# Where the background modulation products of layer 1 are placed: in mLSTM's heads, in the output gate and ahead of the output projection

## The chip, the cores and the metric

The kernel runs on one core of a Trainium2 chip. The metric is the device time of one execution in microseconds (us); a lower time is better. A profiled execution leaves a trace: for each engine (TensorE as PE, its weight loads as PEld, VectorE as DVE, ScalarE as ACT, GpSimd as POOL, SyncE's DMA queue as SP) every instruction with its start, its length and what released it. "L153" is line 153 of the kernel.

## What is computed

The reference is a two-layer trunk over 256 latent and 256 context tokens of width 1024. Only what matters here:

```python
sh1, sc1, g1, sh2, sc2, g2 = adaln(c, ada_w[i], ada_b[i])            # silu(c) @ ada_w[i] + ada_b[i], for each layer i
csh1, csc1, cg1, csh2, csc2, cg2 = adaln(c_ctx, ada_w[i], ada_b[i])  # the same for the context's condition
h = rms_norm(x, norm_mix[i]) * (1.0 + sc1) + sh1                     # hc likewise
# layer 0
mq, mk, mv, mo, mg, aq, ak, av = split(h @ ev_w_in)                  # one input projection
ml = mlstm_bidir(...)                                                # 4 heads of width 128, both directions
y = concat([mlstm_output(ml, mo, ml_norm), gqa(...)]) @ ev_w_out     # output gate, then the output projection
x = x + g1 * y
x = x + g2 * hier_moe(rms_norm(x, norm_ffn[i]) * (1.0 + sc2) + sh2)  # 16 experts, 2 for each token
# layer 1: S5 and SSD heads instead of mLSTM and attention, then the same kind of MoE
```

The modulation products `silu(c) @ ada_w` need nothing of the tokens. `ada_w` is 1024 x 6144 for each layer, 25 MB in float32, and takes part in one product with two rows.

## The kernel before

All 512 tokens lie in four tiles of 128 (`NT` = 4). Layer 0 (`layer0`, `even`) runs in stages: input projections of attention and gates, attention, the mLSTM gates, the queries and keys (four blocks), the values (two blocks of 256 columns, "the value stage"), mLSTM, the output gate (two blocks of 256 columns), `fin` (norm and transposes of mLSTM's output), and the output projection (`out_proj0`). Weights of the input projections are loaded in halves of 512 KB into tiles of the tag `w` (L379, five slots), copied on ScalarE to a high part `wh` (L381) and subtracted on VectorE to a low part `wl` (L383), both with two slots; each product is then three matmuls (L87 to L89).

In mLSTM each of the four heads first builds, for both directions, a table of weights from the gates (L533 on PE, L541 and L544 on DVE, the exponential L549 on ACT). It lies in slots of the tag `x` for even heads and in slots of `wh` for odd heads (L534). Then come the score products (L554), their multiplication into the table (L559), the sums over the values (L567) and the normalisation (L569 to L576).

The modulation products are a background generator, `bgw`: layer 0's second and third part (`ada_b(0)`), layer 1's first part (`ada_a(1)`), layer 1's second and third part (`ada_b(1)`). Each part has 16 steps: a step issues one load of `ada_w` of 512 KB into a slot of `w` (L144), and every second step also issues the products of the last two loads (L153), which go into one PSUM tile. Behind the 16 steps of a part of `ada_b` one more step finishes the part: bias on VectorE (L201), four transposes (L208), copies (L212), and a store to DRAM by POOL (L214). There are 84 steps in all. `bg(n)` takes the next n steps, at a raised priority. The tuple `EVEN_BG` says how many at each place, in order: after each of three blocks of the attention and gate projection, after each of four blocks of queries and keys, after each of the two blocks of values, after each of the two blocks of the output gate. `bg()` without a number, between `fin` and the output projection, takes all that is left.

What sets the order: the DMA queue of SP is issued exactly as the program is written (`manual_schedule`), and a load waits in it until its slot is free; the loads behind it wait with it. The instructions of the other engines are ordered by the planner of the tile framework when the kernel is built: by priority, at the time at which it reckons their inputs to be there. On the chip each engine then runs in that fixed order. The tags `hT` (four slots: the modulated input, read by every projection, later mLSTM's transposed output and a block of `w_out`) and `m8` (four slots: queries, keys, values, mLSTM's output; later a block of `w_out`) also take part in the output projection: `out_proj0` loads the first and second block of `w_out` through `w` into `wh` and `wl`, the third into `hT`, the fourth into `m8`.

With the tuple of before, the steps fall so: 1 to 38 in the blocks up to queries and keys, 39 to 50 in the value stage (the end of `ada_a(1)`), 51 to 62 in the output gate, 63 to 84 ahead of the output projection.

Of the kernel before, what the change touches and what calls it, by code (L numbers as in the profile page):

```python
# [325 lines left out]
def e_pieces(d, sb):  # L326

    if d == 0:
        return [(0, sb, 4)]
    return [[(1, 0, 1), (None, 2, 4)], [(0, 0, 4)], [(1, 2, 3)], [(0, 2, 4)]][sb]  # L330


def pairs(d, tb):

    if d == 0:
        return list(range(tb + 1))
    return [[0, 1], [1], [0, 1, 2, 3], [0, 1, 3]][tb]


class Even(Net):  # L340
# [179 lines left out]
            nc.scalar.activation(cols[:, 1, :, d, :], pv[:, 1, :, d, 0:4], AF.Exp)  # L520
        return cols, nM

    def mlstm(self, cols, nM, qT, kT, v1, hh):
        nc = self.nc
        ss = self.sm.tile([128, NT, ML_H], F32, name="mss", bufs=1)
        scr = self.t("scr", [128, 128])
        for h in range(ML_H):
            W = []
            for d in range(2):
                pm = self.ps(tag="a")  # L530
                r = 32 * d + h
                for z in range(2):
                    nc.tensor.matmul(pm, self.identr[:, r:r + 1].to_broadcast([36, 128]), nM[z], start=(z == 0), stop=(z == 1))  # L533
                w = self.const.tile([128, 1280], F32, name=self.nm("mW"), tag="x", bufs=2) if h % 2 == 0 else self.t("wh", [128, 1280])  # L534
                off, where, offs = 0, {}, {}
                for sb in range(4):
                    for m, a, b in e_pieces(d, sb):
                        n = (b - a) * 128
                        o, i0 = w[:, off:off + n], pm[:, a * 128:b * 128]
                        if m is None:  # L540
                            nc.vector.tensor_scalar(o, i0, cols[:, 0, sb, d, h:h + 1], 0.0, op0=ALU.add, op1=ALU.min)  # L541
                        else:
                            mk = (self.m0, self.m1)[d][:, m * 128:m * 128 + n]
                            nc.vector.scalar_tensor_tensor(o, i0, cols[:, 0, sb, d, h:h + 1], mk, op0=ALU.add, op1=ALU.min)  # L544
                        offs[sb, a] = off
                        for tb in range(a, b):
                            where[sb, tb] = off + (tb - a) * 128
                        off += n
                self.lastW = nc.scalar.activation(w[:, :off], w[:, :off], AF.Exp)  # L549
                W.append((w, offs, where))  # L550
            for sb in range(4):
                t0 = 0 if sb < 2 else 256
                s = self.ps([128, T - t0], "a")
                nc.tensor.matmul(s, kT[:, h, sb * 128:(sb + 1) * 128], qT[:, h, t0:T], start=True, stop=True)  # L554
                for d in range(2):
                    w, offs, _ = W[d]
                    for _, a, b in e_pieces(d, sb):
                        n, off = (b - a) * 128, offs[sb, a]
                        nc.vector.tensor_mul(w[:, off:off + n], w[:, off:off + n], s[:, a * 128 - t0:b * 128 - t0])  # L559
            for tb in range(4):  # L560
                pn = self.ps([128, 2, 129], "b")
                for d in range(2):
                    w, _, where = W[d]
                    ks = pairs(d, tb)
                    for j, sb in enumerate(ks):
                        o = where[sb, tb]
                        self.lastP = nc.tensor.matmul(pn[:, d, :], w[:, o:o + 128], v1[:, sb, h, 0:129], start=(j == 0), stop=(j == len(ks) - 1))  # L567
                den = self.sm.tile([128, 3, 2], F32, name=self.nm("den"), tag="den", bufs=4)
                nc.vector.tensor_scalar(den[:, 0, :], pn[:, :, 128], -1.0, None, op0=ALU.mult)  # L569
                nc.vector.tensor_tensor(den[:, 1, :], den[:, 0, :], pn[:, :, 128], op=ALU.max)  # L570
                nc.vector.tensor_tensor(den[:, 0, :], den[:, 1, :], cols[:, 1, tb, :, h], op=ALU.max)
                nc.vector.reciprocal(den[:, 2, :], den[:, 0, :])
                t = self.t("s2", [128, 128])
                nc.scalar.activation(t, pn[:, 0, 0:128], AF.Copy, scale=den[:, 2, 0:1])
                nc.vector.scalar_tensor_tensor(hh[:, tb, h, :], pn[:, 1, 0:128], den[:, 2, 1:2], t, op0=ALU.mult, op1=ALU.add)
                nc.scalar.activation(scr, hh[:, tb, h, :], AF.Square, accum_out=ss[:, tb, h:h + 1])  # L576

        def fin(mixM):
            v = self.sm.tile([128, NT, ML_H], F32, name="mv", bufs=1)
            nc.vector.tensor_scalar(v, ss, 1.0 / 128, EPS, op0=ALU.mult, op1=ALU.add)  # L580
            r = self.sm.tile([128, NT, ML_H], F32, name="mr", bufs=1)
            self.rsqrt(r, v)
            for tb in range(4):
                p = self.ps(tag="b")
                for h in range(ML_H):
                    nc.vector.tensor_scalar(hh[:, tb, h, :], hh[:, tb, h, :], r[:, tb, h:h + 1], None, op0=ALU.mult)
                    nc.tensor.transpose(p[:, h * 128:(h + 1) * 128], hh[:, tb, h, :], self.ident)
                self.split(mixM[0][:, :, tb * 128:(tb + 1) * 128], mixM[1][:, :, tb * 128:(tb + 1) * 128],
                           p.rearrange("p (h t) -> p h t", h=4))
        return fin  # L590

    def even(self, hT, bg):

        nc, src = self.nc, self.a["ev_w_in"][0]
        bg = iter(bg)
# [22 lines left out]
        cols, nM = self.ml_gates(gp)  # L618
# [4 lines left out]
        qT = self.t("m8", [128, ML_H, T])  # L623
        kT = self.t("m8", [128, ML_H, T])
# [11 lines left out]
        v1 = self.t("m8", [128, NT, ML_H, 130])  # L636
# [6 lines left out]
                nc.vector.tensor_copy(v1[:, i, 2 * c:2 * c + 2, 0:128], p.rearrange("p (h d) -> p h d", h=2))  # L643
            self.bg(next(bg))
        hh = self.t("m8", [128, NT, ML_H, 128])
        fin = self.mlstm(cols, nM, qT, kT, v1, hh)
        for c in range(2):
            w = self.in_w(src, 1536 + 256 * c, 1792 + 256 * c)
            for i in range(NT):
# [54 lines left out]
    def layer0(self):  # L704
        with self.phase("E", dict(ps=2, a=2, b=2, o=1, d=1), wh=2, wl=2), self.sub("Eh", hT=4), \
# [12 lines left out]
            self.bgw = chain(self.ada_b(0), self.ada_a(1), self.ada_b(1))  # L718
            mix = self.even(self.h1T(self.h1_tiles(), xT, *self.shsc[0]), EVEN_BG)
            self.out_proj0(mix)  # L720


EVEN_BG = (4, 4, 6, 6, 6, 6, 6, 6, 6, 6, 6)


def rope_table():
# [1475 lines left out]
```

## Time and profile before

| | us |
|---|---|
| median of three runs | 1331.38 (1319.96 to 1343.16) |
| the profiled execution | 1328.82 |
| its span, first to last instruction | 1327.2 |
| mean granted TensorE clock | 0.927 |
| PE busy in the span | 1137.6 |
| DVE busy in the span | 605.8 |

A table of stretches gives, for a stretch of the span, the busy time and number of instructions of each engine, the granted TensorE clock as a share of full speed, the mean busy share of the 16 DMA engines and what they moved. A row of a timeline gives start and length in us, engine, line, operation, output and inputs, how many instructions are merged in it, and in brackets the idle time of the engine before it and what ended it. Waits name who waited, for whom, the total, how many times, and the longest.

### The profile page before, as it was taken

The page shows a single profiled execution, that of the slowest core. Times are in us where ns is not written, and L with a number is a line of the kernel's source. Part 1 is how long each engine was busy: PE and PEld are TensorE (multiplying, and loading weights), DVE is VectorE, ACT ScalarE, POOL GpSimd, SP SyncE. Part 2 cuts the span into 40 slices and gives each one's busy share as a digit, 9 for nine tenths or more (in the row PEclk, how much of TensorE's full clock was granted, in tenths as well). Part 3 has the DMA queues.
Part 4 walks back from the last instruction along what each step waited for, and adds up shares of the span by engine and source line. Part 5 has one row for each costly group of instructions (what it writes and reads, how often), then busy time and mean ns, then how long its engine had stood idle before and what let it go on. Part 6 is the DMA issues. An engine that isn't in the chain of part 4 may idle for free. (4 is left out here: it accounts for less than half of the span.)

```text
span 1327.2 us, 23457 instructions
## 1 busy us (share of the span) xinstructions
PE 1137.6 (86%) x9689; PEld 701.2 (53%) x9689; DVE 605.8 (46%) x1647; ACT 304.1 (23%) x590; POOL 130.0 (10%) x185
## 2 busy tenths in 40 slices
PE   3899998977879599999999966967867789999895
PEld 0575564656579345545665525846756643432221
DVE  2657664186247521837013188799631531211112
ACT  2425441034121111111121134346221211110000
POOL 2002020000300251212101100000000000000000
PEclk8999999999989699999999986988767889999998
DMA  7876136703993899999999742342769859999960
GB/s 275 281 269 237 50 129 223 252 2 120 320 289 123 277 309 363 348 388 352 367 337 335 280 160 66 112 112 61 289 88 199 360 203 412 420 420 420 420 256 34
DMA packets 103973, 330.40 MB, mean 249 GB/s; under 512 B 18049, under 2 KB 56089, under 8 KB 78256
## 3 DMA queue, kind: packets, MB, share of 16 engines
q1 hardware_dynamic: 94592, 298.98, 63.2%
q0 software_dynamic: 9264, 29.81, 7.1%
q8 instruction: 80, 1.31, 0.4%
q14 instruction: 37, 0.30, 0.1%
HBM read 312.68 MB, written 18.01 MB: 249 GB/s over the span
## 5 line engine op out<-in xcount | busy, mean ns | idle before, releaser
L981 PE MATMUL ps<-wa,xT 128*32 128x512 f32 x848 | 167.2, 599 | 0.0
L981 PE MATMUL ps<-wb,xT 128*32 128x512 f32 x608 | 139.3, 594 | 0.0
L87 PE MATMUL ps<-wh,hT 128*128 128x256 f32 (+2 forms) x320 | 93.9, 294 | 6.5 <-ACT wh L381 4.7
L89 PE MATMUL ps<-wh,hT 128*128 128x256 f32 (+2 forms) x320 | 93.1, 293 | 4.0 <-DVE hT L315 4.0
L153 PE MATMUL ps<-w,cT 128*32 128x512 f32 x384 | 67.7, 782 | 28.2 <-DMA w<-in_ada_w_dram 24.2
L88 PE MATMUL ps<-wl,hT 128*128 128x256 f32 (+2 forms) x288 | 83.3, 290 | 1.4 <-DVE wl L383 1.4
L984 PE MATMUL ps<-wa,xT 128*32 128x256 f32 x496 | 82.9, 381 | 0.0
L984 PE MATMUL ps<-wb,xT 128*32 128x256 f32 x480 | 82.3, 380 | 0.0
L989 ACT ACTIVATE s<-ps 64x512 f32<-64x512 f32 (+1 forms) x48 | 23.4, 516 | 247.1 <-PE ps L981 246.6
L87 PE MATMUL ps<-hT,wh 128*128 128x512 f32 (+1 forms) x160 | 61.6, 385 | 14.4 <-DVE xs L1722 11.5
L87 PEld LDWEIGHTS ps<-wh,hT 128*128 128x128 f32 x320 | 62.6, 196 | 15.2 <-issue 6.1
L89 PEld LDWEIGHTS ps<-wh,hT 128*128 128x128 f32 x320 | 62.3, 196 | 15.5 <-issue 8.5
L981 PEld LDWEIGHTS ps<-wa,xT 128*32 128x32 f32 x848 | 45.0, 110 | 37.9 <-issue 24.7
L88 PE MATMUL ps<-hT,wh 128*128 128x512 f32 (+1 forms) x160 | 60.6, 379 | 0.0
L89 PE MATMUL ps<-hT,wl 128*128 128x512 f32 (+1 forms) x160 | 60.2, 377 | 0.2 <-DVE wl L1643 0.2
L88 PEld LDWEIGHTS ps<-wl,hT 128*128 128x128 f32 x288 | 55.2, 192 | 7.8 <-issue 5.9
L970 DVE COPY xT<-ps 128x384 f32<-128x384 f32 x16 | 8.9, 556 | 105.9 <-PE ps L984 98.3
L981 PEld LDWEIGHTS ps<-wb,xT 128*32 128x32 f32 x608 | 38.6, 110 | 21.8 <-issue 7.7
L1027 POOL DMA_INDIRECT yd<-y,si x30 | 34.5, 1149 | 155.6 <-ACT y L1018 150.2
L1275 DVE COPY aT<-ps 128x256 f32<-128x256 f32 x16 | 6.8, 424 | 89.3 <-PE ps L1273 89.3
L981 PE MATMUL ps<-wc,xT 128*32 128x512 f32 x288 | 46.5, 595 | 0.0
L87 PEld LDWEIGHTS ps<-hT,wh 128*128 128x128 f32 x160 | 31.8, 199 | 23.5 <-issue 15.7
(659 smaller groups left out, 2387.9 us busy)
## 6 DMA issues: line engine op xcount, KB each, us to landing
w<-in_ada_w_dram SPq DMA_DIRECT2D x96, 512.0 KB
wa<-in_moe_w_down_dram SPq DMA_DIRECT2D x30, 1024.0 KB
wa<-in_moe_w_up_dram SPq DMA_DIRECT2D x28, 1024.0 KB
wa<-in_moe_w_gate_dram SPq DMA_DIRECT2D x25, 1024.0 KB
wb<-in_moe_w_gate_dram SPq DMA_DIRECT2D x21, 1024.0 KB
wb<-in_moe_w_down_dram SPq DMA_DIRECT2D x17, 1024.0 KB
wb<-in_moe_w_up_dram SPq DMA_DIRECT2D x16, 1024.0 KB
w<-in_ev_w_in_dram SPq DMA_DIRECT2D x16, 512.0 KB
```

Of the source, the lines that this page charges most:

```text
L87: mm(p, x[0], y[0], start=first, stop=False)
L88: mm(p, x[0], y[1], start=False, stop=False)
L89: return mm(p, x[1], y[0], start=False, stop=last)
L153: o, i = nc.tensor.matmul(p[32 * q:32 * q + 32, :], self.cT[:, k, :], rhs, start=(k == 0), stop=(k == KD - 1)), o
L970: nc.vector.tensor_copy(xT[:, 0:4, :], p)
L981: self.up = nc.tensor.matmul(P[32 * j:32 * j + 32, :], xT[:, k, 32 * (j % 2):32 * (j % 2) + 32], (wg, wu)[j // 2](k), start=(k == 0), stop ...
L984: nc.tensor.matmul(Q[32 * j:32 * j + 32, :], xT[:, k, 64:96], (wg, wu)[j // 2](k)[:, (j % 2) * 256:(j % 2) * 256 + 256], start=(k == 0), s ...
L989: nc.scalar.activation(s, p[0:64, :], AF.Silu)
L1027: st = self.nc.gpsimd.indirect_dma_start(out=rows, out_offset=bass.IndirectOffsetOnAxis(ap=idx, axis=0), in_=y, in_offset=None, bounds_che ...
L1275: nc.vector.tensor_copy(aT, tr)
```

## The change

The function `mlstm` gets the iterator over `EVEN_BG` and takes background steps in each head, after the tables of both directions and before the score products. The tuple has four more entries: six steps in each of the four heads, then four instead of six after each block of the output gate. The steps up to the value stage are as before (1 to 50); 51 to 74 now fall in mLSTM, 75 to 82 in the output gate, and the last two ahead of the output projection. Steps 67 and 84 are the finishing steps of layer 1's second and third part.

```diff
-    def mlstm(self, cols, nM, qT, kT, v1, hh):
+    def mlstm(self, cols, nM, qT, kT, v1, hh, bg):
...
                 self.lastW = nc.scalar.activation(w[:, :off], w[:, :off], AF.Exp)
                 W.append((w, offs, where))
+            self.bg(next(bg))
             for sb in range(4):
...
-        fin = self.mlstm(cols, nM, qT, kT, v1, hh)
+        fin = self.mlstm(cols, nM, qT, kT, v1, hh, bg)
...
-EVEN_BG = (4, 4, 6, 6, 6, 6, 6, 6, 6, 6, 6)
+EVEN_BG = (4, 4, 6, 6, 6, 6, 6, 6, 6, 6, 6, 6, 6, 4, 4)
```

## Rows read from the trace of the kernel before

**Rows 1.** The page's group of the modulation products: busy, mean ns, idle before, releaser.

```profile
L153 PE MATMUL ps<-w,cT 128*32 128x512 f32 x384 | 67.7, 782 | 28.2 <-DMA w<-in_ada_w_dram 24.2
```

**Rows 2.** Table of stretches: mLSTM, a part of it, the gate, the projection's start.

```profile
core 0: us, PE busy (x) PEld busy (x) DVE busy (x) ACT busy (x) POOL busy (x), PEclk, DMA share, GB/s
266.00:316.10 50.10, 39.34 (x207) 29.57 (x205) 39.86 (x148) 20.55 (x52) 0.00 (x0) 0.93 0.00 1
277.00:288.00 11.00, 10.18 (x50) 7.84 (x49) 8.29 (x32) 4.41 (x11) 0.00 (x0) 0.84 0.00 0
316.10:355.00 38.90, 35.86 (x279) 25.62 (x279) 12.77 (x40) 8.71 (x18) 15.29 (x22) 1.00 0.85 288
363.00:377.00 14.00, 7.78 (x37) 5.91 (x29) 5.28 (x7) 3.14 (x3) 1.17 (x2) 0.51 1.09 312
```

**Rows 3.** Timeline of SP's queue from 220 to 380 us.

```profile
233.22 4.69 SPq L379 DMA_DIRECT2D w<-in_ev_w_in_dram  x2
238.00 18.39 SPq L144 DMA_DIRECT2D w<-in_ada_w_dram  x6
256.49 5.03 SPq L379 DMA_DIRECT2D w<-in_ev_w_in_dram  x2
261.62 97.46 SPq L144 DMA_DIRECT2D w<-in_ada_w_dram  x26
...
360.17 17.26 SPq L379 DMA_DIRECT2D w<-in_ev_w_out_dram  x12
```

**Rows 4.** Waits of SP's queue from 262 to 320 us.

```profile
SPq L144 <- DVE den L572: 55.5, 1, 55.5
```

**Rows 5.** Timeline of PE in the value stage: the modulation products.

```profile
247.43 1.07 PE L153 MATMUL ps<-w,cT 128*32 128x512 f32 x8
...
254.95 1.07 PE L153 MATMUL ps<-w,cT 128*32 128x512 f32 x8 [2.84 <-DMA w<-in_ada_w_dram]
...
260.04 1.06 PE L153 MATMUL ps<-w,cT 128*32 128x512 f32 x8 [0.43 <-DMA w<-in_ada_w_dram]
```

**Rows 6.** Groups by line of PE from 316.5 to 353.6 us.

```profile
L153 PE MATMUL ps<-w,cT 128*32 128x512 f32 x72 | 9.6, 604 | 1.6 <-DMA w<-in_ada_w_dram 1.6
```

**Rows 7.** Timeline of PE from the gate's first product to the projection's first matmul.

```profile
322.94 1.06 PE L153 MATMUL ps<-w,cT 128*32 128x512 f32 x8 [1.39 <-DMA w<-in_ada_w_dram]
...
353.62 0.49 PE L587 MATMUL ps<-ident,m 128*128 128x128 f32 x3
...
362.65 1.53 PE L153 MATMUL ps<-w,cT 128*32 128x512 f32 x8 [2.37 <-DMA w<-in_ada_w_dram]
...
365.71 1.11 PE L208 MATMUL ps<-ident,ab 128*128 128x128 f32 x4 [1.53 <-DVE ab L205]
...
370.83 0.58 PE L87 MATMUL ps<-wh,hT 128*128 128x256 f32 x1 [4.01 <-ACT wh L381]
```

**Rows 8.** Timeline of DVE: the finishing of a part, and the splits after the gate.

```profile
338.30 0.68 DVE L201 TENSOR_TENSOR ab<-ab,ps 128x512 f32<-128x512 f32 x1
...
356.31 1.28 DVE L82 TENSOR_TENSOR hT<-ps,hT 128x512 fp32r<-128x512 f32 x2
...
359.94 0.69 DVE L82 TENSOR_TENSOR hT<-ps,hT 128x512 fp32r<-128x512 f32 x1 [0.89 <-ACT hT L81]
```

**Rows 9.** Waits of PE from 363 to 500 us.

```profile
PE ps L966 <- DMA xg<-h2d,gi: 5.7, 1, 5.7
PE ps L87 <- ACT wh L381: 5.1, 2, 4.0
...
PE ps L88 <- DVE wl L383: 1.6, 2, 0.9
```

**Rows 10.** Timeline of PE in mLSTM's third and fourth head: the sums.

```profile
300.49 5.03 PE L567 MATMUL ps<-m,mW 128*128 128x129 f32 x28 [1.29 <-DVE m L575]
...
307.95 0.94 PE L567 MATMUL ps<-m,wh 128*128 128x129 f32 x6 [0.71 <-DVE m L575]
...
312.66 3.39 PE L567 MATMUL ps<-m,wh 128*128 128x129 f32 x28 [1.77 <-DVE m L575]
```

## The prediction

> **What bounds the kernel now.** I first read the page: the modulation products (L153) are a small part of TensorE's work, but of its costly groups the one whose idle time is put down to a weight load [rows 1]. Then the table of stretches: in mLSTM (266 to 316.1 us) the DMA engines move nothing and PE is idle for 10.8 of 50.1 us; in the output gate (316.1 to 355) DMA is at 0.85 and PE all but full; in 363 to 377 DMA is saturated and PE half idle at a granted clock of 0.51 [rows 2]. The order of SP's queue says why. The output gate's weights are issued at 233.22 and 256.49, then one load of `ada_w` at 261.62, and the other 25 of that batch only after a stall [rows 3]. The stall is one wait of 55.5 us for a slot of `w` [rows 4]: four of its five slots hold output-gate weights, whose split copies need `wh`, which the odd heads of mLSTM occupy to the end. The fifth slot holds half a pair.
>
> A pair, below, is two loads of 512 KB and their eight matmul records (two for each matmul of the source), 1.07 us of PE. Before mLSTM three pairs of layer 1's second modulation part run [rows 5], though their products are written behind mLSTM: the planner already carries a product as far forward as its loads allow, so the place in SP's queue decides. The other 13 pairs run afterwards: nine (72 records) between 316.5 and 353.6 [rows 6], four up to 364, the last of them at 362.65 [rows 7]. Only then have `w_out`'s loads been issued, at 360.17 [rows 3], and the output projection starts at 370.83, after a wait of 4.01 us for the copy that such a load feeds [rows 7].
>
> **The change, step by step.** It changes no work, only the place of loads and pairs: 24 background steps (23 loads) go into mLSTM, 8 instead of 12 into the output gate, 2 (one load) instead of 22 ahead of the projection. In SP's queue the gate's loads now stand behind 23 more loads of `ada_w`, and `w_out`'s behind one.
>
> (a) *From the end of the gate's matmuls to the projection.* Today 353.62 to 370.83 = 17.2 us [rows 7]. It holds four pairs, a wait of 2.37 for a load, 1.53 and 1.11 for the transposes of the finished part, and the 4.01. What must stay is the split of the gated token blocks on VectorE: the first ends at 357.0 (356.31 plus half of 1.28), the last at 360.63 [rows 8], so 3.4 to 7.0 us. One block is enough for the first matmul; I take 3.7: **-13.5** (-13.8 to -10.2).
>
> (b) *Output gate.* Nine pairs, 9.6 us, lie in it [rows 6]. How many remain? After mLSTM's 23 loads SP has: gate weights (2), 4 loads, gate weights (2), 4, then 1. As today, four gate halves and a load that lacks its partner will fill the five slots and SP will stop; so 27 loads go out before the stop and 5 after it, and 3 pairs remain, 3.2 us. The first wait of 1.39 [rows 7] stays, the other 0.2 of 1.6 [rows 6] goes: **-6.6** (-4.5 with two more pairs left, -9.8 with none).
>
> (c) *Early projection.* TensorE waits 5.1 us for two copies, of which 4.01 is in (a), and 1.6 for two subtractions [rows 9], so 2.7 beyond (a). In 363 to 377 it computes 7.78 us at a clock of 0.51 [rows 2], of which 1.2 is the last pair and 1.1 the transposes; the other 5.5 would be 2.8 at 1.00. With `w_out`'s loads out by 330 or so, up to 5.4 us could go, but the second block's copy and subtraction still need slots that the gate reads to its end: **-2.5** (0 to -5.4).
>
> (d) *The value stage, up to 266.* Loads go on from 233.22 without the gate's weights in between, which took SP until 238.00 [rows 3], and with all five slots; so the first pair can come 4.8 us before today's 247.43 [rows 5]. In the gate, nine pairs from 322.94 to 353.6 are one in 3.4 us [rows 6, 7]. From 242.6 to 269 that is 8 pairs instead of 3. PE is saturated there apart from load waits of 2.84 and 0.43 [rows 5], so five pairs cost 5.4 in full; the waits go, since the slots no longer stop the loads: **+2.1** (0 to +5.4).
>
> (e) *mLSTM.* 16 - 8 - 3 = 5 pairs, 5.3 us of PE. Ahead of its runs of L567 a head has waits of 1.29 (1.77 in the last) and 0.71 us [rows 10], in which a pair can hide; elsewhere a pair holds up a chain in which VectorE and TensorE wait for each other, VectorE being busy 39.86 of 50.1 us [rows 2]. I take half, 2.7, plus the 0.68 of L201 [rows 8], a VectorE addition at the end of a part, which now falls there: **+3.4** (-2.6, the pairs hidden and the second rival's gain, to +6.0).
>
> Queues: POOL, which loads a part's bias and stores the part, does nothing in mLSTM [rows 2], and neither does DMA. The diff leaves the order of PE and DVE to the planner. Behind the projection nothing swallows an earlier start: the first expert product waits 5.7 us for the gather of its tokens, not for weights [rows 9].
>
> Sum: -13.5 - 6.6 - 2.5 + 2.1 + 3.4 = -17.1 us. The profiled execution takes 1328.82 us, its span 1327.2 and the rest around it; that gives 1311.7. The median of the runs is 2.6 us higher, which would give 1314; I put the forecast at **1312**.
>
> **The rivals.**
>
> *Little gain.* The pairs cost their full time, and the projection's weights come late: (d) +5.4, (e) +6.0, (a) -10.2, (b) -6.6, (c) 0, together -5.4, **1324**. For it: VectorE's 39.86 of 50.1. Against: the waits of 1.29 and 0.71, and DMA idle for 50 us.
>
> *More gain.* The pairs vanish in mLSTM's waits and PE keeps its clock. Of two runs of 28 records of L567 one took 3.39 us and one 5.03, after a wait of 1.29 [rows 10]; the granted clock is 0.84 on the mean of 277 to 288 [rows 2], where another such run lies, so part of it at 1.2 and not 2.4 GHz. Two runs give back 3.3. Then (e) is 0.7 - 3.3 = -2.6, (d) 0, (c) -5.4: with (a) and (b) -28.1, **1301**. The Trainium skill (TensorE: Matmul & The Clock Gate, Part 1) says that half rate is the resting state and that activity lifts it; by that rule denser work in mLSTM would bring this case. The trace agrees as far as the slow run follows a pause, but the run of 3.39 follows a longer one of 1.77 and is not slow.
>
> *Slower.* PE runs in order: a pair whose load is late stops mLSTM's matmuls behind it, and VectorE with them. At the dearest such wait, 2.84 us [rows 5], for all 10 pairs moved it is 28.4 on top of the forecast, **1340**. It decides from 17.1 / 10 = 1.7 us for a pair. Against: with the loads queued without gaps, the gate's nine pairs waited 1.6 us in all [rows 6]. The same page (Part 3, The mechanism) says that matmuls start and end strictly in program order, which speaks against this change; the waits in front of L153 agree, since nothing overtakes them.
>
> *No effect.* The projection's start is held by something else, such as `w_out`'s last two blocks, which go into slots that the gate reads to its end, or the five slots of `w` move the stall elsewhere: **1329**. For it: the gate's weights still fill four slots until mLSTM ends; against: only five loads of `ada_w` are left then.
>
> That all 12 pairs of the 23 loads run in the value stage is no rival: PE pays 10 x 1.07 = 10.7 there, less 3.3, and (e) is 0, 2 us more than the forecast.
>
> **How the numbers follow.** Forecast 0.52 (its own range 1304 to 1319), little gain 0.20, more gain 0.16, slower 0.06, no effect 0.06. The range 1300 to 1326 holds the forecast, little gain and most of more gain. Two per cent, about what a measurement of this kernel tells from no change, is 26.6 us: faster means below 1304.8, where more gain and a little of the forecast lie, 0.19; slower means above 1358, 0.02; between, 0.79.
>
> **What would show it.** After mLSTM about five loads of `ada_w` instead of 25; about eight pairs before mLSTM, five in it, three after; mLSTM at most 7 us longer than 50; the projection within 4 us of the gate's last matmul, with `w_out` issued before 335. If L554 or L567 stand behind waits for `ada_w`, or mLSTM grows by over 12 us, (e) is wrong; if the projection still waits over 2 us for a copy, (a) is.

## The result, and the profile after

The changed kernel takes 1309.84 us (median of four runs, 1302.33 to 1314.74) against 1330.08 for the kernel before in the same comparison (four runs, 1319.96 to 1343.16). The ratio is 0.9861, with a 95% interval of 0.982 to 0.9903: faster by 1.4%, which the interval tells apart from no change, and less than the 2% that the prediction used as a bound. The profiled execution takes 1311.75 us; the forecast was 1312. The lines of the changed kernel are one higher than before from L550 on (L567 is now L568).

SP's queue shows the change itself. These are its loads from 218 to 354 us in the kernel after:

```profile
218.05 4.73 SPq L379 DMA_DIRECT2D w<-in_ev_w_in_dram  x2
222.88 52.56 SPq L144 DMA_DIRECT2D w<-in_ada_w_dram  x29
278.03 0.93 SPq L379 DMA_DIRECT2D w<-in_ev_w_in_dram  x2
281.64 8.62 SPq L144 DMA_DIRECT2D w<-in_ada_w_dram  x4
294.16 0.93 SPq L379 DMA_DIRECT2D w<-in_ev_w_in_dram  x2
321.21 5.08 SPq L144 DMA_DIRECT2D w<-in_ada_w_dram  x5
...
327.32 26.61 SPq L379 DMA_DIRECT2D w<-in_ev_w_out_dram  x12
```

Where [rows 3] had six loads of `ada_w` between the gate's weights and 26 behind them, 29 now run ahead of them (six for the steps of the value stage, 23 for those of mLSTM), four between, and five are left when the stall ends. `w_out` begins to go out at 327.32 instead of 360.17. The stall of [rows 4] is there still, behind the same instruction, but at under half its length, and it now falls where only five loads stand behind it (waits of SP's queue, 240 to 345 us):

```profile
SPq L144 <- DVE den L573: 26.1, 1, 26.1
```

PE's products of `ada_w` in the value stage, mLSTM and the gate (timeline of PE):

```profile
246.30 1.06 PE L153 MATMUL ps<-w,cT 128*32 128x512 f32 x8
...
257.00 1.07 PE L153 MATMUL ps<-w,cT 128*32 128x512 f32 x8 [0.41 <-DMA w<-in_ada_w_dram]
...
288.34 1.06 PE L153 MATMUL ps<-w,cT 128*32 128x512 f32 x8 [1.10 <-DMA w<-in_ada_w_dram]
...
293.05 1.07 PE L153 MATMUL ps<-w,cT 128*32 128x512 f32 x8
...
332.59 1.06 PE L153 MATMUL ps<-w,cT 128*32 128x512 f32 x8 [0.81 <-DMA w<-in_ada_w_dram]
```

Seven pairs stand in the value stage (246.30 to 267.28), six in mLSTM (270.40 to 293.05), three in the gate, none behind it; the forecast was 8, 5 and 3. The sums of mLSTM that answer to [rows 10]:

```profile
305.39 3.39 PE L568 MATMUL ps<-m,mW 128*128 128x129 f32 x28 [1.29 <-DVE m L576]
...
315.91 3.39 PE L568 MATMUL ps<-m,wh 128*128 128x129 f32 x28 [1.77 <-DVE m L576]
```

Both take 3.39 us here; the first was 5.03 before. Then the end of the gate and the start of the projection, which answer to [rows 7]:

```profile
348.75 1.03 PE L588 MATMUL ps<-ident,m 128*128 128x128 f32 x8
350.86 0.38 PE L87 MATMUL ps<-wh,hT 128*128 128x256 f32 x1 [1.08 <-ACT hT L81]
...
352.71 0.39 PE L88 MATMUL ps<-wl,hT 128*128 128x256 f32 x1 [1.23 <-DVE wl L383]
...
353.72 0.36 PE L89 MATMUL ps<-wh,hT 128*128 128x256 f32 x1
```

The projection starts 2.1 us after the gate's last product instead of 17.2. Two rows of the table of stretches, mLSTM and the gate, stand against [rows 2]; the granted clock is 1.00 in both:

```profile
269.29:319.30 50.01, 42.97 (x261) 28.32 (x260) 40.78 (x151) 20.51 (x52) 5.41 (x9) 1.00 0.52 171
319.30:348.75 29.45, 27.14 (x222) 23.89 (x222) 15.82 (x42) 10.38 (x19) 12.43 (x16) 1.00 0.95 267
```

Routing, the first work of layer 0's MoE that waits for every token, starts 23.3 us earlier (the products L867, then L868, by line; first and last start are the two numbers ahead of the semicolon). First the kernel before:

```profile
L867 PE MATMUL ps<-sel,ones x13: 174/174/175, 446.8 to 1064.9; 128*128 128x16 bf16 x13
```

and after:

```profile
L868 PE MATMUL ps<-sel,ones x13: 173/174/177, 423.5 to 1046.3; 128*128 128x16 bf16 x13
```

But the end comes only 17.1 us earlier (span 1327.2 and 1310.1). Of 23.3 us, 6.9 are given back in the experts of that MoE, where the change moves no work: from the first to the last transposed token block they last 456.1 to 727.0 = 270.9 us before, and 432.8 to 710.6 = 277.8 after. The waits of PE in this stretch say where. Before:

```profile
PE ps L966 <- DVE xT L970: 3.9, 5, 1.2
```

After:

```profile
PE ps L967 <- DVE xT L971: 8.2, 5, 5.3
PE ps L967 <- DMA xg<-h2d,gi: 5.6, 1, 5.6
```

The wait for the gather is that of [rows 9]; the one for the copy of tokens on VectorE has grown, by a single wait of 5.3 us. VectorE's timeline shows what stands ahead of that copy. Before:

```profile
487.11 0.18 DVE L1383 TENSOR_SCALAR ea<-s5ld 128x32 f32<-128x32 f32 x1 [8.99 <-DMA s5ld<-in_s_log_dt_dram]
...
491.90 0.56 DVE L970 COPY xT<-ps 128x384 f32<-128x384 f32 x1 [1.45 <-PE ps L984]
```

After:

```profile
469.01 0.46 DVE L1384 TENSOR_SCALAR ea<-s5ld 128x32 f32<-128x32 f32 x1 [15.00 <-DMA s5ld<-in_s_log_dt_dram]
...
472.40 0.55 DVE L971 COPY xT<-ps 128x384 f32<-128x384 f32 x1
```

L1384 belongs to layer 1: it begins the table of an exponential (`exp_acc`), and its input `s5ld` comes with two small loads that POOL issues at the start of layer 0's MoE (`odd_loads`, L1443). In VectorE's fixed order this table stands ahead of the copy of the fourth expert's tokens. Before, the load lands early enough that the copy still waits 1.45 us for PE; after, it lands later, and PE waits for the copy.
The Trainium skill (TensorE: Matmul & The Clock Gate, Part 1, Architectural detail) says that VectorE takes its work strictly first in, first out. The trace agrees: the copy starts 3.4 us after the table's first instruction, and not during the 15.00 us ahead of it.

### The profile page after: what moved, and what is told of

Its sections match the earlier page's. It is cut to its first block, busy times and chain, and to the rows that moved or that the text cites. A ratio compares the mean times of both kernels' runs of the same rounds, so it can differ in the third digit from the quotient of the medians.

```text
span 1310.1 us, 23459 instructions
## 1 busy us (share of the span) xinstructions
PE 1132.7 (86%) x9689; PEld 694.0 (53%) x9689; DVE 605.2 (46%) x1647; ACT 304.1 (23%) x590; POOL 131.0 (10%) x185
## 5 line engine op out<-in xcount | busy, mean ns | idle before, releaser
L87 PE MATMUL ps<-wh,hT 128*128 128x256 f32 (+2 forms) x320 | 93.7, 294 | 3.6 <-ACT hT L298 1.8
L89 PE MATMUL ps<-wh,hT 128*128 128x256 f32 (+2 forms) x320 | 92.4, 291 | 4.0 <-DVE hT L315 4.0
L153 PE MATMUL ps<-w,cT 128*32 128x512 f32 x384 | 67.2, 777 | 25.2 <-DMA w<-in_ada_w_dram 20.9
L87 PE MATMUL ps<-hT,wh 128*128 128x512 f32 (+1 forms) x160 | 61.5, 384 | 14.2 <-DVE xs L1723 11.6
L89 PEld LDWEIGHTS ps<-wh,hT 128*128 128x128 f32 x320 | 61.8, 194 | 14.5 <-issue 7.7
L87 PEld LDWEIGHTS ps<-wh,hT 128*128 128x128 f32 x320 | 62.4, 195 | 11.3 <-issue 6.1
L89 PE MATMUL ps<-hT,wl 128*128 128x512 f32 (+1 forms) x160 | 60.0, 375 | 0.2 <-DVE wl L1644 0.2
L87 PEld LDWEIGHTS ps<-hT,wh 128*128 128x128 f32 x160 | 31.6, 197 | 23.3 <-issue 15.7
```

The lines of the kernel that those rows point to most:

```text
L87: mm(p, x[0], y[0], start=first, stop=False)
L89: return mm(p, x[1], y[0], start=False, stop=last)
L153: o, i = nc.tensor.matmul(p[32 * q:32 * q + 32, :], self.cT[:, k, :], rhs, start=(k == 0), stop=(k == KD - 1)), o
```

## Experiments

Two theories were to be told apart at first: that the stages gain as forecast and the pairs in mLSTM cost about half their time, or that their cost there is full or none; then, with the traces at hand, what the loss in the experts is. The table has the stages of all traces: the end of the value stage, the lengths of mLSTM and gate, the time from the gate's last product to the projection's first, the length of the experts, the pairs in value stage, mLSTM and behind it, and how many of mLSTM's runs of 28 sums, whole or in part, went at half the clock (5.03 instead of 3.39 us).

| kernel | value end | mLSTM | gate | to projection | experts | pairs | runs at half clock |
|---|---|---|---|---|---|---|---|
| before | 265.35 | 50.70 | 37.57 | 17.21 | 270.9 | 3/0/13 | 2 |
| b2_before | 264.42 | 50.70 | 37.32 | 16.86 | 271.2 | 3/0/13 | 2 |
| b3_before | 267.63 | 52.91 | 38.40 | 17.06 | 271.1 | 3/0/13 | 2 to 3 |
| before_copy_first | 264.70 | 50.02 | 37.28 | 16.80 | 271.2 | 3/0/13 | 1 |
| after | 269.29 | 50.01 | 29.45 | 2.11 | 277.8 | 7/6/3 | 0 |
| a2_after | 268.43 | 50.37 | 29.60 | 2.12 | 277.9 | 7/6/3 | 0 |
| a3_after | 269.09 | 51.55 | 28.98 | 2.12 | 273.8 | 7/6/3 | 1 |
| head0 | 269.89 | 51.84 | 29.25 | 2.12 | 275.3 | 7/6/3 | 1 |
| after_copy_first | 268.13 | 51.52 | 28.63 | 2.12 | 270.8 | 7/6/3 | 1 |
| gate_only | 266.87 | 53.62 | 35.38 | 5.50 | 271.6 | 4/4/8 | 2 |
| all_mlstm | 268.27 | 54.43 | 24.44 | 2.70 | 275.4 | 7/9/0 | 1 |
| all_copy_first | 269.12 | 52.86 | 24.44 | 2.79 | 270.8 | 7/9/0 | 0 |
| twice5 | 267.99 | 58.27 | 30.13 | 2.12 | 271.5 | 7/6/3, five twice | 0 |

**Does the place within mLSTM matter? (head0)** All 24 steps are given in the first head.

```
-EVEN_BG = (4, 4, 6, 6, 6, 6, 6, 6, 6, 6, 6, 6, 6, 4, 4)
+EVEN_BG = (4, 4, 6, 6, 6, 6, 6, 6, 6, 24, 0, 0, 0, 4, 4)
```

> All 24 mLSTM steps taken in the first head (24, 0, 0, 0, 4, 4) instead of six in each. Theory: only the place in SP's queue counts, and that queue is the same; the built program has the same instructions in the same order on every engine as the changed kernel, so it is also its second measurement: 0.986 of before, 1305 to 1315 us, seven pairs in the value stage, six in mLSTM, three behind. Rival (the place in the heads matters): not the same stage lengths. On the loss at the MoE's start, chance: the wait of 5.3 us in front of the second expert is 0 to 3 us here; systematic: 4 to 7 us again.

1310.85 us, ratio 0.9846 (0.9787 to 0.9904). The planner puts the pairs where it reckons their loads to be there, and both tuples give the same instructions in the same order on every engine. So "six in each head" is only a way of writing: what counts is that the loads are issued ahead of the gate's weights. The run serves as a repeat of the changed kernel.

**The gate alone. (gate_only)** No steps in mLSTM, 16 after each block of the gate, two steps (one load) left for the place ahead of the projection, as in the changed kernel.

```
+EVEN_BG = (4, 4, 6, 6, 6, 6, 6, 6, 6, 0, 0, 0, 0, 16, 16)
```

> No step in mLSTM, 16 after each block of the output gate, two ahead of the projection: the loads are only moved from behind the gate to within it. Theory (the order in SP's queue decides): 16 loads go out behind the first block's weights with three slots, so about eight pairs run before mLSTM's end, then four slots are held and SP stops; eight pairs remain for the gate and 15 loads stand ahead of w_out instead of five. mLSTM about 50 us, the gate about 5 us longer than in the changed kernel, the projection's start 4 to 8 us later: 1316 to 1322 us, half of the gain. Rival (what counts is that mLSTM itself takes steps): no gain, 1325 to 1333 us.

1318.19 us, ratio 0.9919 (0.9886 to 0.9953). SP's queue in this kernel:

```profile
240.03 40.81 SPq L144 DMA_DIRECT2D w<-in_ada_w_dram  x16
...
286.17 59.21 SPq L144 DMA_DIRECT2D w<-in_ada_w_dram  x16
...
346.47 21.10 SPq L379 DMA_DIRECT2D w<-in_ev_w_out_dram  x12
```

Even without a step in the heads four pairs run in mLSTM, since the first block's 16 loads go out from 240 us on. But the 16 loads behind the second block's weights are caught in the stall, `w_out` follows at 346.47, eight pairs lie behind mLSTM, and the projection waits 5.5 us. All but emptying the place ahead of the projection, with half of the loads ahead of the second block's weights, brings 11 us in the comparison's medians (1329.25 to 1318.19); the other loads ahead of the gate's weights bring the rest.

**All in mLSTM. (all_mlstm)** 34 steps in the heads, none in the gate.

```
+EVEN_BG = (4, 4, 6, 6, 6, 6, 6, 6, 6, 9, 9, 8, 8, 0, 0)
```

> All 34 remaining steps in mLSTM (9, 9, 8, 8), none in the gate or ahead of the projection. Theory: seven or eight pairs in the value stage, eight or nine in mLSTM, none behind it; four gate halves then hold four slots, and w_out's first half the fifth. The gate loses its three pairs (3.2 us) and its wait of 0.8, w_out's loads are issued some 5 us earlier; mLSTM grows by under 1 us a pair: 3 to 5 us less than the changed kernel, 1304 to 1308. Rival (mLSTM has no more room): its length grows by 3 us or more and the gate's gain is given back: 1309 to 1312.

1307.37 us, ratio 0.9829 (0.9774 to 0.9884). No load of `ada_w` is left behind the gate's weights:

```profile
222.34 68.93 SPq L144 DMA_DIRECT2D w<-in_ada_w_dram  x38
...
312.76 37.87 SPq L379 DMA_DIRECT2D w<-in_ev_w_out_dram  x12
```

The gate is 5 us shorter than after, and mLSTM, with nine pairs, 2.9 (all_copy_first) to 4.4 longer. The difference to the changed kernel is within the intervals.

These runs price a pair in mLSTM. With 1.64 us (5.03 less 3.39) taken off for each run at half clock (b3_before, where part of one more is hit, is left out), mLSTM without pairs takes 47.4 to 48.4 us, with six 49.9 to 50.4, with nine 52.8 to 52.9. Six cost 1.5 to 3.0 and nine 4.4 to 5.5, which is 0.25 to 0.6 us a pair of its 1.07, and of the six's cost 1.1 to 1.6 are waits for loads. The four of gate_only cost 2.0 to 3.0, up to 0.75 a pair, but theirs wait 3.3 us for loads.

**Five pairs more. (twice5)** Of layer 1's third part, the products of pairs 1 to 5 are issued twice (640 of the weight's 1024 rows, those whose number leaves 1 to 5 when divided by 8, then count twice in it), with no load added.

```
+                    for _ in range(2 if l == 1 and v == 2 and 1 <= k <= 5 else 1):
                         o, i = nc.tensor.matmul(p[32 * q:32 * q + 32, :], ...), o
```

> The changed kernel with five pairs of products issued twice (rows 128 to 767 of the third modulation part count twice in the product, which is left so): 5 x 1.07 = 5.4 us more of PE, nearly all of it in mLSTM, with no load more. If a pair hides in mLSTM as the stage lengths say (six pairs made it 50.0 and 51.8 us long against 50.7, with one or two runs of the sums at the full clock instead of the half: some 0.4 us a pair), mLSTM is 51 to 54 us, and the kernel 1 to 3 us slower than the changed one. If a pair costs its full time there, mLSTM is 55 to 57 us and the kernel 5 us slower.

mLSTM takes 58.27 us, 7.9 to 8.4 more than with six single pairs at equal clock. Four of the five doubled pairs stand in mLSTM, at 275.62, 279.00, 288.73 and 294.60; the fifth stands in the gate, at 331.78. A doubled pair lasts 1.95 us instead of 1.07, so the four add 3.5 us of products. The rest is not the products' own: two of the doubled pairs stand in PE's order ahead of their loads (timeline of PE in twice5, where L153 is L154):

```profile
288.73 1.95 PE L154 MATMUL ps<-w,cT 128*32 128x512 f32 x16 [2.73 <-DMA w<-in_ada_w_dram]
...
294.60 1.95 PE L154 MATMUL ps<-w,cT 128*32 128x512 f32 x16 [2.02 <-DMA w<-in_ada_w_dram]
...
331.78 1.95 PE L154 MATMUL ps<-w,cT 128*32 128x512 f32 x16
```

Those waits are 4.75 us, against 1.1 to 1.6 with single pairs. Without the difference, 3.1 to 3.7, the doubled products cost 4.2 to 5.3 us: more than all of their time. So the run does not repeat the price of 0.25 to 0.6 a pair. Either the pauses of mLSTM take in the first products and none of the next, or the planner, which orders PE anew around longer products, put them in worse places; the run doesn't tell which. It does show the mechanism of the rival "slower", a late load in an ordered queue, at 2 to 3 us for a pair. Its whole time can't be told from that of the kernel after (1311.87, ratio 0.986, 0.9819 to 0.9901); its experts, at 271.5 us, give back part of what mLSTM loses, and the next point is about that.

**The loss in the experts: chance or the change?** Nothing is moved there, so further executions of the same kernels were profiled.

> The kernel before once more, for a second trace of it. The changed kernel gained 23.3 us up to the routing of layer 0's MoE, but only 16.4 were left behind its first two experts: there the second expert's matmuls waited 5.3 us for a copy that VectorE did late, behind instructions that waited for small loads. Theory A (chance): how late those loads land varies from execution to execution; then this trace has another wait in front of the second expert than the 0.7 us of the first trace, or the next run of the changed kernel has another than 5.3. Theory B (systematic): the kernel before waits under 1.5 us there every time, and its first expert block takes 17.5 us again from one expert's transposes to the next.

> The changed kernel again, one look. The experts' stretch was 277.8 and 275.3 us in its two traces, 270.8 with the edge of order. If the loss belongs to the change, it is 274 us or more again; if it is chance, 270 to 272 here or 274 and more in a trace of before.

> The changed kernel, a further look with the same question: experts' stretch 274 us or more (belongs to the change) or 270 to 272 (chance); mLSTM 50.0 to 51.8 us, with no run or one of the sums at the half clock.

> The kernel before, a third look. If the loss belongs to the change, its experts' stretch is 270 to 272 us once more, with a wait of 1.2 us for the copy; if it is chance, it is sometimes 274 or more. In mLSTM, two runs of the sums at the half clock again (50.7 us) if that follows from the pauses of PE; one or none if it varies.

The whole times were 1322.52 (b2_before), 1310.35 (a2_after), 1302.55 (a3_after) and 1326.82 (b3_before). Before, the experts take 270.9 to 271.2 us in three executions; after, 277.8, 277.9 and 273.8, and 275.3 in head0. The two groups don't meet, so in these traces the loss goes with the change. The wait behind it varies, and follows one quantity: when POOL issues the second load of `s5ld`, counted from the first transposed tokens.

| kernel | second load of `s5ld` issued after, us | longest of that wait of PE, us | experts, us |
|---|---|---|---|
| before | 25.0 | 0.7 | 270.9 |
| b3_before | 26.1 | 1.2 | 271.1 |
| b2_before | 26.4 | 0.7 | 271.2 |
| gate_only | 26.5 | 1.4 | 271.6 |
| twice5 | 26.8 | 1.6 | 271.5 |
| all_mlstm | 27.8 | 2.8 | 275.4 |
| a3_after | 27.8 | 3.2 | 273.8 |
| head0 | 28.0 | 2.8 | 275.3 |
| after | 30.3 | 5.3 | 277.8 |
| a2_after | 30.8 | 5.5 | 277.9 |

Up to about 26.8 us next to nothing is lost; from there PE waits a us for each us. The stretch doesn't lose just the wait: against the kernel before it is 6.9 us longer for a wait of 5.3 in the kernel after, 4.5 for 2.8 in all_mlstm and 2.9 for 3.2 in a3_after. Behind the wait the granted clock is 0.78 over 20 us in the kernel after, against 1.00 behind the same copy before (table of stretches, before and then after; 0.83 in all_mlstm, 0.91 in a3_after):

```profile
492.50:512.50 20.00, 19.43 (x215) 11.97 (x218) 3.53 (x7) 2.10 (x5) 5.91 (x9) 1.00 1.01 358
```

```profile
472.75:492.75 20.00, 19.75 (x189) 9.13 (x192) 2.21 (x5) 1.06 (x2) 6.93 (x11) 0.78 0.89 305
```

**Take away what makes the copy wait. (before_copy_first, after_copy_first, all_copy_first)** The first instruction of the table is told to come behind the copy of the fourth expert's tokens, in VectorE's order alone; no work changes. In the edit, `hold` is that copy (`xTc`).

```
+                self.xTc = self.ao[-1] if len(self.gat) == 3 else getattr(self, "xTc", None)
...
-        nc.vector.tensor_scalar(t[0], x, -87.0, 87.0, op0=ALU.max, op1=ALU.min)
+        self.after(nc.vector.tensor_scalar(t[0], x, -87.0, 87.0, op0=ALU.max, op1=ALU.min), *hold)
```

> The changed kernel with one edge of order more: VectorE's work on layer 1's tables, which waits for small loads that POOL issues at the MoE's start, is put behind its copy of the fourth expert's tokens instead of ahead of it. Theory: the changed kernel loses up to 7 us there (its stretch from the first to the last token transposes of the experts was 277.8 and 275.3 us in two traces, 271.0 and 271.2 in the kernel before), because VectorE stands in that wait while the copy is ready; then PE's wait for the copy (5.3 and 2.8 us) falls under 1.5, the clock stays at 1.00, and the stretch is 270 to 272 us: 4 to 6 us less than the changed kernel, 1303 to 1308. Rival (the loss is in the weights' loads, which compete with the small ones): another wait takes its place, the stretch stays at 275 to 278, 1308 to 1312.

> The same edge of order in the kernel before. Theory: its two traces show waits of only 1.2 us there, so there is nothing to gain: 0.997 to 1.003 of before, stretch 270 to 272 us. If it gains 4 us or more, the loss belongs to both kernels and varies by chance, and the two traces of before were lucky.

> All 34 steps in mLSTM together with the edge of order. Theory: both gains add: 1300 to 1305, 0.980 of before or less; mLSTM 53 to 55 us, the gate 24 to 25, the stretch of the experts 270 to 272. Rival: the stretch stays at 275, 1304 to 1309.

VectorE in after_copy_first; the copy comes first, and the table's start no longer matters to PE:

```profile
470.42 0.56 DVE L971 COPY xT<-ps 128x384 f32<-128x384 f32 x1 [7.28 <-PE ps L987]
471.95 0.17 DVE L1386 TENSOR_SCALAR ea<-s5ld 128x32 f32<-128x32 f32 x1
```

And PE's waits in its experts:

```profile
PE ps L967 <- DVE xT L971: 3.3, 4, 1.2
```

The second `s5ld` load goes out 29.5 us after the first tokens here, as late as in the changed kernel, and the experts take 270.8 us. The changed kernel with this edit takes 1302.0 us (ratio 0.9823, 0.9758 to 0.9888). That is 7.8 below the changed kernel's median, but the two stem from different comparisons, and by their ratios (0.9823 and 0.9861, whose intervals overlap) it is 5 us. From the last token block to its end the kernel, with nothing moved there, takes anything from 588.7 to 600.4 us in these traces. What shows the effect is the experts' length, 3.0 to 7.1 us shorter than in the traces of the changed kernel, and not the whole time. The kernel before gains nothing from it that can be told (1327.48, ratio 0.9981, 0.9942 to 1.002), as its three traces lose nothing there. But in before_copy_first the second `s5ld` load goes out 27.9 us after the first tokens, 2.9 us later than in the trace of before, and 2.1 of these are there at 472.41, ahead of the first instruction that the edit moves (482.11). By the table above PE would have waited some 3 us for so late a load in the unedited order (an estimate), so the kernel before isn't safe from the loss either. So the loss is VectorE's order together with the late load, and it is mended without touching the change. With all steps in mLSTM as well it takes 1299.94 us (ratio 0.9786, 0.9723 to 0.985), the lowest median of the study.

Why the small loads come later can be followed one step back. POOL issues them in order behind other small loads, some of which wait for expert weights (`wb`) or a gather (`xg`) to land. POOL's timeline before:

```profile
471.15 0.82 POOL L1442 DMA_DIRECT2D LL<-in_s_b_im_dram  x1 [1.67 <-DMA wb<-in_moe_w_down_dram]
472.47 0.81 POOL L1442 DMA_DIRECT2D LL<-in_s_b_im_dram  x1 [0.50 <-DMA xg<-h2d,gi]
```

and after:

```profile
445.62 0.82 POOL L1443 DMA_DIRECT2D LL<-in_s_b_im_dram  x1 [1.04 <-DMA wb<-in_moe_w_down_dram]
449.32 0.82 POOL L1443 DMA_DIRECT2D LL<-in_s_b_im_dram  x1 [2.88 <-DMA wb<-in_moe_w_down_dram]
452.73 0.82 POOL L1443 DMA_DIRECT2D LL<-in_s_b_im_dram  x1 [2.58 <-DMA xg<-h2d,gi]
```

These waits are 2.2 us before and 6.5 after, 4.3 of the 5.3 us by which the second `s5ld` load is later in this pair of traces (30.3 less 25.0). Why the weights and the gather land later in the kernel after, relative to the first tokens, stays open; no run moved them.

## Why the prediction came out, point by point

The steps against the traces; the last column has the means of the four traces of the kernel before (before_copy_first is the same up to the experts) and of five of the kernel after (with head0 and after_copy_first). For the experts the kernels with the VectorE edit are left out.

| step | forecast | the two profiled executions | means |
|---|---|---|---|
| (d) up to the end of the value stage | +2.1 (0 to +5.4) | +3.9 | +3.4 |
| (e) mLSTM | +3.4 (-2.6 to +6.0) | -0.7 | 0.0 |
| (b) gate | -6.6 (-9.8 to -4.5) | -8.1 | -8.5 |
| (a) gate's end to projection | -13.5 (-13.8 to -10.2) | -15.1 | -14.9 |
| (c) projection | -2.5 (-5.4 to 0) | -3.3 | -1.9 |
| sum up to routing | -17.1 | -23.3 | -21.8 |
| the experts | 0 | +6.9 | +5.1 |

**The number was right by two errors that cancel, which is luck.** The sum up to routing was 5 to 6 us too small, most of it in (e), and the sentence "Behind the projection nothing swallows an earlier start" was wrong: the experts swallow 5 to 7. It rested on [rows 9], PE's waits up to 500 us in the kernel before. They show the gather's 5.7 us rightly, but PE's wait for the copy is only 0.7 us long before, and its length doesn't tell that it is on the edge. What would have shown it is VectorE's timeline: an instruction that waits 8.99 us for a small load, five us ahead of a copy that PE needs. What the experts give back, put at nothing, is the term that failed.

**(a)** was mis-sized, 3.7 us where 2.1 was measured. I took half of VectorE's split of the first token block for the condition. The first matmul (L87) needs the high part alone, which ScalarE's L81 gives; only L89 needs the split, and comes at 353.72, 5 us after the gate's end. It lies a little outside its bounds.

**(b)** had the mechanism and the number of pairs right: five loads behind the stall, three pairs. Six pairs fewer are 6.4 us and the waits for loads fall from 1.6 to 0.8. The other 0.9 us comes from the gate's own 192 matmuls. From each start to the next, without waits, they take 25.2 us with nine pairs among them (before), 23.9 with three (after) and 23.0 with none (all_mlstm), and a pair takes 1.00. So in the gate, where PE is all but full, a pair costs some 1.24 us, 0.24 of it in the matmuls beside it.

**(c)** lies within its bounds, but its size is mostly the clock. From its first matmul to routing the projection's stretch takes 75.3 to 76.2 us in the four traces of the kernel before, and after 72.7 (after, a2_after), 74.0 (a3_after) and 75.3 (head0, after_copy_first). In its first 15 us the granted clock is 0.77 to 0.85 before, and after 1.00, 0.89 and 0.77 in that order. The waits for copies and subtractions, of which 2.7 us were to go, are still 1.4 in the kernel after.

**(d)** was counted as 8 pairs against 3 and is 7, the first at 246.30, one in about 3.5 us, as the nine of [rows 6, 7] had been. Of the 3.9 us between the two traces 2.0 were there long before it: a pair of an earlier stage starts at 224.81 instead of 222.76 (1.1 of the 3.4 on the mean). The other 1.9 are the stage's own: four pairs more are 4.3 us, and the waits for their loads fall from 3.3 [rows 5] to 0.4.

**(e)** The half was a fair guess for the pairs: at equal clock the stage grows by 1.5 to 3.0 us with six pairs, where 3.4 was forecast with five. But in the two profiled executions mLSTM got shorter, since the kernel before had two runs of sums at half the clock and the one after none: 3.3 us, as the rival "more gain" had it. The size of that varies from execution to execution: head0, a3_after and after_copy_first, which run the same order up to there, each have one such run. But it isn't chance alone: the four traces of the kernel before have seven or eight of them, the five of the kernel after three, and the first run of 28 in mLSTM, slow in three of the four, is at the full clock in all of the five. On the mean that is about 2 us, as much as the pairs cost, and it was left out of the forecast's -17.1. Whether the pairs keep the clock up there no run was made to tell. The Trainium skill (TensorE: Matmul & The Clock Gate, Part 1) says that the clock's monitor runs freely and doesn't reset when the kernel starts, so that one kernel can show different numbers of matmuls at the lower rate, at its start, from run to run. The traces show such a difference in the middle of one kernel, with 0 such runs of sums in after and a2_after and 1 in a3_after.

**The rivals.** "No effect" is out by the projection's start, 2.1 us behind the gate and not 17.2. "Slower" has its mechanism in twice5 alone; in the kernel after, all waits of PE for `ada_w` from the value stage to the gate are 2.3 us, 0.15 for each of 16 pairs and far from the 1.7 from which it decides. "Little gain" is out by (a), 15.1 us where it had 10.2, and by the pairs' price in mLSTM, though (d) lies halfway to its +5.4. "More gain" had the clock of mLSTM's sums right in the two profiled executions, but not its sum: the pairs are not free, and the stages up to routing gave 23.3 us (21.8 on the mean), halfway between 17.1 and its 28.1. The two kernels with the VectorE edit, 1302.0 and 1299.94, come near its 1301 by another cause.

**What would show it.** Five loads after mLSTM, `w_out` before 335 and the projection within 4 us all came. L555 and L568 don't stand behind a wait for `ada_w` longer than 1.43 us in the traces of the kernel after.

## What to carry to other kernels

When a long stage is made earlier, look behind it for every engine's instruction that waits for a load, not only for waits of the engine that bounds: in a fixed order, an instruction of later work whose small load is just in time becomes a stall of the work behind it as soon as the front moves. Where a queue in strict order holds loads of two kinds, their order counts: with all but one of the loads taken out of the place ahead of the projection, the projection came 11.7 us closer to the gate when 16 of these loads still stood behind the gate's weights (gate_only), and 15.1 when five did. And when a forecast comes out, compare the stages before trusting it; a sum can be right over two wrong terms.

## What the hardware showed beyond that

The same kernel, in the same order, gets another clock in another execution. In head0 the granted clock falls to 0.50, which is 1.2 GHz, as the projection starts with gaps (table of stretches, PE busy 1.04 of 2 us in the first, saturated in the second):

```profile
354.00:356.00 2.00, 1.04 (x3) 0.75 (x4) 2.00 (x3) 1.43 (x2) 0.00 (x0) 0.64 0.82 174
356.00:358.00 2.00, 2.00 (x12) 2.00 (x11) 1.90 (x4) 1.30 (x2) 0.00 (x0) 0.50 0.80 193
```

Over the first 15 us of its projection it is 0.77, while the kernel after, with the same instructions, has

```profile
350.86:365.86 15.00, 13.56 (x113) 13.15 (x114) 12.99 (x23) 7.50 (x13) 0.14 (x1) 1.00 0.72 191
```

that is 1.00. This, with the runs of sums, is worth some 1.6 to 3 us a place, about as much as the terms (c), (d) and (e); a single pair of traces doesn't settle terms of that size, and that is why the table above has means.
